# Order edges for the norms' small TensorE products, and a PSUM bank for one column half, in a two-layer decoder trunk

## The chip, the cores and the metric

The kernel runs on one core of a Trainium2 chip. The metric is the device time of one execution in microseconds. Before the change the median of three runs was 1242.19 us (1241.92 to 1243.76).

## The reference

The model has two layers on 512 tokens plus 16 learned meta tokens (528 columns in all), with a model width of 1024. Everything is float32 at the interface. Each layer does, cut to what matters here:

```
h = h + rmsnorm( mixer(rmsnorm(h, pre_mix)),  post_mix )
h = h + rmsnorm( conv_ffn(rmsnorm(h, pre_ffn)), post_ffn )

mixer(x):    proj = x @ w_in  (1024 x 3600); a retention group (4 heads) and a gated
             linear attention group (4 heads) work on its columns;
             both results, normalised and gated, side by side, then @ w_out (1024 x 1024)
conv_ffn(x): u = x @ ffn_up (1024 x 5632); a causal width-3 convolution per column;
             (gelu(first half) * second half) @ ffn_down (2816 x 1024)
rmsnorm(x, w): x * rsqrt(mean(x*x over the width) + 1e-6) * w
```

The output is h without the meta tokens. A norm is over the width, and the width lies on the partitions in this kernel, so each token's sum of squares runs across partitions.

## The kernel before, in words

**Layout.** Activations are kept transposed: 8 tiles of 128 rows (the width), with the 528 tokens along the columns. Columns are cut into two halves, 0 to 232 and 232 to 528 (`SPLIT` is 232; the second half has 296 columns). In the last layer the first half begins at column 14 for what only the tokens' own outputs need, so it has 218 columns.

**Large products.** A float32 product is made of three fp16 products: weights and activations are split into a high and a low part, and `product_step` issues high*high (L469), high*low (L470) and low*high (L471) into the same PSUM accumulator. `product` runs `product_step` over the 8 row tiles (22 in the down-projection). An accumulator is one tile of a pool of three PSUM banks (`mm`); a second pool (`mx`) has the other five. The profile names these accumulators `pj` (input projection), `po` (output projection), `pu` (up-projection), `pp` (paired up-projection) and `pd` (down-projection). The rank-16 gate projection has its own step, `rank_step` (L727). Weights come by DMA into a stage and are split by ScalarE (L120) and VectorE (L124), about ten units ahead of their use.

**Norms.** `norms` runs once for each column half behind the output projections of both layers and behind the first layer's down-projection: six times. While the product's tiles are evacuated, `sumsq` squares them on ScalarE and adds the squares (L435, GpSimd or VectorE) into `acc`, 128 partitions of partial sums. Then `token_rstd` works in two small steps on TensorE:

- `nst` (L419): two or three products of a slice of `acc` with a column of ones give each token's sum; VectorE scales it and adds epsilon (L402), GpSimd raises it to the power -0.5 (L403);
- `nbc` (L643): VectorE makes a diagonal of the result (`ndg`, L647), and a product of ones with this diagonal spreads it over all partitions.

In fp32 each such product shows as two in the profile (four or six in a group). Between the two calls of `token_rstd`, eight passes on VectorE (L448), GpSimd (L450) and ScalarE add the normalised result to the residual `h` and collect the squares of the new `h`. After the second call, `scaled` and `split` write the next stage's input `xh` (`every` in the profile): its high part by ScalarE (L407), its low part by VectorE (L408). So a norm has four small groups on TensorE, in a chain with the other engines between them.

**What sets the order.** The first part of the kernel (to the first nine tiles of the first mixer) is in a region whose order is that of the program. Behind it, a planner writes each engine's order before the run. It goes by its own model of durations, and each time an engine is free in that model it takes, among the instructions whose inputs the model calls ready, the one that stands first in the program. In the program, a half's `norms` is written out whole as soon as that half's products are: so the four small groups stand before all the products of the next half, and the planner puts each where its model has its input ready. On the chip every engine then works strictly through the written order.

**The last block.** The last down-projection (`last_down`) works on blocks of 128 tokens and 512 output columns with a Strassen-like scheme: seven products (`w11`, `t1`, `t2`, `w22`, `t3`, `w21`, `t4`) with sums of the inputs and of the weights, into PSUM accumulators `pa`, `pb` and `pd` of one bank each (L1324). The last product, `t4`, is added to `pa[0]` for token block 2, and then to `pa[1]` for token block 3, in two column halves of 256. Behind each half, ScalarE squares it (L1392) and VectorE multiplies it with the gains (L1396). The products of the second half write the same bank that these two read, so the framework makes them wait. At the end come the scaled sum (L1397), the power (L1398), four passes of VectorE that scale and add the residual (L1401; `hp` is the residual, transposed by TensorE at L1363) and four output transfers (L1402), on SyncE's and ScalarE's queues in turn. Block 2's own end is `result` (L1342 to L1345) and `final` (L1349 to L1353).

## Time and profile before

| | |
|---|---|
| median of the runs | 1242.19 us (1241.92 to 1243.76) |
| the profiled execution's own time | 1243.79 us |
| its span in the trace | 1241.7 us |
| TensorE busy (matmuls) | 1221.0 us, 98% |
| VectorE busy | 838.9 us, 68% |
| ScalarE busy | 667.5 us, 54% |
| GpSimd busy | 160.0 us, 13% |
| share of TensorE in the chain that ended last | 90% |

PE is TensorE (PEld its weight loads), DVE VectorE, ACT ScalarE, POOL GpSimd, SP SyncE; a q behind a name is the engine's sequencer. A timeline row gives the start, the duration, the engine and line, the operation, the output and input tiles, the shape and the count of instructions merged into it; a bracket at its end gives the engine's idle time before it and what ended that. A row of the waits gives the engine and line, what it waited for, the total in us, how often, and the longest. Matmuls overlap, so the duration of one (0.29 us for 296 columns) is longer than the distance to the next.

### The profile page before, as it was taken

What the parts mean: (1) busy time and instruction counts of PE and PEld (TensorE: products, weight loads), DVE (VectorE), ACT (ScalarE), POOL (GpSimd) and SP (SyncE); (2) the same over time, 40 slices, a digit from 0 to 9 for tenths busy, and PEclk for the clock granted to TensorE, in tenths of its full rate; (3) what the DMA queues carried; (4) which work ended last, traced back from release to release, by engine and by line L of the source; (5) the groups of instructions that cost most, each with busy time, mean ns of one, the idle gap of its engine ahead of it and who ended that gap; (6) DMA issues with size and microseconds to landing.
All of it is one profiled execution on the core that took longest, in us unless ns stands there. A gap on an engine that the chain in (4) does not pass through costs nothing.

```text
span 1241.7 us, 26411 instructions
## 1 busy us (share of the span) xinstructions
PE 1221.0 (98%) x11079; PEld 1013.5 (82%) x11079; DVE 838.9 (68%) x1485; ACT 667.5 (54%) x1316; POOL 160.0 (13%) x205
## 2 busy tenths in 40 slices
PE   8999999999999999999999999999999999999997
PEld 7778888988888888988887788889798888886444
DVE  5677745467998777623465777443769768887686
ACT  5674445454776666523335654453648556664442
POOL 1012311153000000000220223011520000000001
PEclk9999999999999999999999999999999999999999
DMA  7932121131423333424243232212314333304461
GB/s 202 273 102 86 60 79 52 52 97 40 136 70 110 100 97 96 119 73 108 63 114 98 69 86 70 69 52 69 104 51 136 102 103 103 119 2 170 160 239 68
DMA packets 207275, 124.18 MB, mean 100 GB/s; under 512 B 6880, under 2 KB 194836, under 8 KB 207156
## 3 DMA queue, kind: packets, MB, share of 16 engines
q1 hardware_dynamic: 206708, 121.71, 33.7%
q8 instruction: 87, 1.43, 0.5%
q0 software_dynamic: 160, 0.52, 0.1%
q14 instruction: 32, 0.26, 0.1%
q10 hardware_dynamic: 288, 0.26, 0.1%
HBM read 120.38 MB, written 2.10 MB: 99 GB/s over the span
## 4 chain that ended last, share of the span: by engine, by line
PE 90%; ACT 3%; DVE 3%; issue 1%; POOL 1%; DMA 0%; SPq 0%; POOLq 0%; DVEq 0%; ACTq 0%
PE pu L470 11%; PE pu L471 11%; PE pu L469 11%; PE pl L1324 8%; PE pj L469 7%; PE pj L471 7%; PE pj L470 7%; PE pp L1145 3%; PE pd L470 3%; PE pd L471 3%; PE pd L469 3%; PE po L469 2%; PE po L471 2%; PE po L470 2%; PE o L776 1%
## 5 line engine op out<-in xcount | busy, mean ns | idle before, releaser
L470 PE MATMUL pu<-every,unit 128*128 128x296 f16 (+2 forms) x1248 | 341.2, 274 | 2.1 <-DVE every L408 2.1
L471 PE MATMUL pu<-every,unit 128*128 128x296 f16 (+2 forms) x1248 | 341.2, 274 | 0.0
L469 PE MATMUL pu<-every,unit 128*128 128x296 f16 (+2 forms) x1248 | 339.6, 274 | 0.7 <-ACT every L407 0.7
L471 PEld LDWEIGHTS <-unit 128*128 128x128 f16 x2700 | 264.4, 98 | 44.2 <-issue 3.8
L469 PEld LDWEIGHTS <-unit 128*128 128x128 f16 x2700 | 264.6, 98 | 43.9 <-issue 3.9
L470 PEld LDWEIGHTS <-unit 128*128 128x128 f16 x2700 | 264.8, 98 | 39.0 <-issue 0.6
L124 DVE SCALAR_TENSOR_TENSOR unit<-st,unit 128x1024 f16<-128x1024 f32 (+1 forms) x173 | 212.0, 1227 | 100.7 <-ACT unit L120 100.0
L471 PE MATMUL pj<-every,unit 128*128 128x296 f16 (+2 forms) x888 | 244.8, 276 | 0.9 <-DVE unit L124 0.9
L469 PE MATMUL pj<-every,unit 128*128 128x296 f16 (+2 forms) x888 | 245.1, 276 | 0.5 <-DVE room L933 0.5
L470 PE MATMUL pj<-every,unit 128*128 128x296 f16 (+2 forms) x888 | 244.9, 276 | 0.0
L120 ACT ACTIVATE unit<-st 128x1024 f16<-128x1024 f32 (+1 forms) x171 | 177.9, 1041 | 75.1 <-PE pu L471 21.2
L1201 ACT ACTIVATE u<-pu 128x296 f32<-128x296 f32 (+2 forms) x156 | 58.5, 378 | 72.6 <-PE pu L471 72.6
L435 DVE TENSOR_TENSOR acc<-acc,sq 128x296 f32<-128x296 f32 (+2 forms) x60 | 33.4, 558 | 77.6 <-ACT sq L433 75.7
L471 PE MATMUL pd<-av,unit 128*128 128x232 f16 (+1 forms) x308 | 84.7, 276 | 0.0
L470 PE MATMUL pd<-av,unit 128*128 128x232 f16 (+1 forms) x308 | 84.7, 276 | 0.0
L469 PE MATMUL pd<-av,unit 128*128 128x296 f16 (+1 forms) x308 | 84.5, 276 | 0.0
L403 POOL TENSOR_TENSOR every<-every 128x5 f32<-128x5 f32 (+6 forms) x31 | 38.1, 1229 | 295.7 <-DVE every L402 250.4
L1324 PE MATMUL pl<-unit,fk 128*128 128x512 f16 x330 | 71.4, 379 | 0.0
L1190 DVE SCALAR_TENSOR_TENSOR cg<-u,every,cg 128x527 f32<-128x527 f32 (+1 forms) x88 | 66.4, 754 | 5.0 <-ACT cg L1185 4.3
L471 PE MATMUL po<-merged,unit 128*128 128x296 f16 (+2 forms) x256 | 69.7, 274 | 0.0
L470 PE MATMUL po<-merged,unit 128*128 128x296 f16 (+2 forms) x256 | 69.7, 274 | 0.0
L469 PE MATMUL po<-merged,unit 128*128 128x296 f16 (+2 forms) x256 | 69.4, 274 | 0.0
(260 smaller groups left out, 1745.7 us busy)
## 6 DMA issues: line engine op xcount, KB each, us to landing
st<-in_ffn_up SPq DMA_DIRECT2D x78, 512.0 KB, 3.8
st<-in_w_in SPq DMA_DIRECT2D x56, 512.0 KB, 4.6
st<-in_ffn_down SPq DMA_DIRECT2D x46, 512.0 KB, 3.9
st<-in_w_out SPq DMA_DIRECT2D x16, 512.0 KB, 3.6
st<-in_ffn_up SPq DMA_DIRECT2D x20, 256.0 KB, 4.0
st<-in_ffn_down SPq DMA_DIRECT2D x8, 384.0 KB, 3.4
xt<-in_x SPq DMA_DIRECT2D x6, 256.0 KB, 6.2
w<-in_ffn_down SPq DMA_DIRECT2D x3, 512.0 KB, 4.3
```

The source lines that it names most:

```text
L120: self.kern.nc.scalar.activation(self.u[:, 0], self.st, AF.Copy, scale=SW)
L124: self.kern.nc.vector.scalar_tensor_tensor(out=self.u[:, 1, ks], in0=self.st[:, ks], scalar=SW, in1=self.u[:, 0, ks], op0=ALU.mult, op1=AL ...
L403: nc.gpsimd.tensor_tensor(out=r[:w, :n], in0=t[:w, :n], in1=self.mhalf[:w, :n], op=ALU.pow)
L435: eng.tensor_tensor(out=acc[:, :n], in0=acc[:, :n], in1=sq[:, :n], op=ALU.add)
L469: nc.tensor.matmul(ps[:, :n], w[:, 0, kk, :], x[:, 0, n0:n1], start=first, stop=False)
L470: nc.tensor.matmul(ps[:, :n], w[:, 0, kk, :], x[:, 1, n0:n1], start=False, stop=False)
L471: nc.tensor.matmul(ps[:, :n], w[:, 1, kk, :], x[:, 0, n0:n1], start=False, stop=last)
L776: nc.tensor.matmul(o[:, i, :], intra(i), vn(i), start=i == 0, stop=i == 0, skip_group_check=i > 0)
L1145: mm = lambda p, q, **kw: nc.tensor.matmul(ps, u[:, p, k, :], x[k][:, q], skip_group_check=more, **kw)
L1190: nc.vector.scalar_tensor_tensor(out=to, in0=u[:, max(lo, d) - d : L - d], scalar=self.cvec[:, ci(i) : ci(i) + 1], in1=to, op0=ALU.mult, o ...
L1201: nc.scalar.activation(u[:, n0:n1], ps[:, : n1 - n0], AF.Copy, scale=IXW)
L1324: mm = lambda x, w, **kw: nc.tensor.matmul(ps[:, cols], x, w[:, cols], skip_group_check=more, **kw)
```

## The change

Two edits.

*Marks.* A clock counts the columns of the large products in the order of the program: `product_step` adds three times its columns, `rank_step` its columns. At the start of `norms`, four places on this clock are set: 2.2, 3.5, 2.6 + 66*n/2340 and 3.5 us apart, at 2340 columns per us, where n is the half's number of columns. When the clock has passed a place, the first matmul of that `product_step` gets an edge to the last matmul of the small group that belongs to the place: it must come behind it in TensorE's order. The edge is for the planner; it makes no semaphore.

*The last block.* The first column half of `t4` for token block 3 goes to a bank of its own, `pe`, the third of the pool `mm`. What `pa[1]` held in these columns is copied to SBUF beforehand (`done`) and added by VectorE when the half is evacuated. The square of this half is taken from SBUF, and its product with the gains is a pass of its own. The order of the last few steps is written anew: the scaled sum and the power come before the last half's product with the gains, and the last passes are one of 512 columns and two of 256, with three output transfers.

```diff
+PER_US = 2340
...
         self.gated, self.credit, self.beat = [], [0.0, 0.0], 0
+        self.clock, self.marks = 0.0, []
...
-    def token_rstd(self, acc, n0, n1, out):
+    def token_rstd(self, acc, n0, n1, out, at_sum, at_spread):
...
         for i, c0 in enumerate(at):
-            nc.tensor.matmul(st[:w, i : i + 1], acc[:, c0 : c0 + w], self.ones[:, :1], start=True, stop=True)
+            one = nc.tensor.matmul(st[:w, i : i + 1], acc[:, c0 : c0 + w], self.ones[:, :1], start=True, stop=True)
+        self.marks.append((at_sum, one))
         r = self.rstd(st[:w, :nk], nk, 1.0 / D, EPS, w)
         yield
         bc = self.mx([P, WN], "nbc")
         for i, c0 in enumerate(at):
-            self.spread(bc[:, c0 : c0 + w], r[:w, i : i + 1], w)
+            one = self.spread(bc[:, c0 : c0 + w], r[:w, i : i + 1], w)
+        self.marks.append((at_spread, one))
         out.append(bc)
...
-        yield from self.token_rstd(acc, n0, n1, out)
+
+        at, ways = [self.clock], (PER_US * 2.2, PER_US * 3.5, PER_US * 2.6 + 66 * n, PER_US * 3.5)
+        for way in ways:
+            at.append(at[-1] + way)
+        yield from self.token_rstd(acc, n0, n1, out, at[1], at[2])
...
-        yield from self.token_rstd(acc2, n0, n1, out)
+        yield from self.token_rstd(acc2, n0, n1, out, at[3], at[4])
...
+    def after_marks(self, ins, n):
+
+        while self.marks and self.marks[0][0] <= self.clock:
+            self.tc.add_manual_dep(ins.ins, self.marks.pop(0)[1].ins.name,
+                                   mybir.DependencyInfo(mybir.DependencyClass.NoSync, mybir.DependencyReason.DATA), reason="marks")
+        self.clock += n
+
     def product_step(self, ps, w, kk, x, n0, n1, first, last):
         nc = self.nc
         n = n1 - n0
-        nc.tensor.matmul(ps[:, :n], w[:, 0, kk, :], x[:, 0, n0:n1], start=first, stop=False)
+        one = nc.tensor.matmul(ps[:, :n], w[:, 0, kk, :], x[:, 0, n0:n1], start=first, stop=False)
+        self.after_marks(one, 3 * n)
...
     def rank_step(self, ps, u, k, n0, n1):
         for i in range(2):
+            self.clock += n1 - n0
...
+        done = self.g([P, 512], F32, "part")[:, :256]
+        nc.scalar.activation(done, pa[1][:, :256], AF.Copy, scale=IAW)
+        pe = self.mm([P, 512], "pl")
         pd = banks(self.mx)
         multiply(("w21", av["x12"], pd, False))
...
-        half, sums = [slice(0, 256), slice(256, 512)], self.ss
-        for i, cols in enumerate(half):
-            multiply(("t4", av["x22"], {1: pa[1]}, True), cols=cols)
-            sq = self.g([P, 512], F32, "sqo")[:, cols]
-            nc.scalar.activation(sq, pa[1][:, cols], AF.Square, scale=IAW, accum_out=sums[:, i : i + 1])
-            if i == 0:
-                nc.vector.tensor_tensor(out=sums[:, 2:3], in0=sums[:, 0:1], in1=ss[:, 7:8], op=ALU.add)
-                nc.vector.tensor_scalar(out=sums[:, 3:4], in0=sums[:, 2:3], scalar1=1.0 / D, scalar2=EPS, op0=ALU.mult, op1=ALU.add)
-            nc.vector.scalar_tensor_tensor(out=ys[3][0][:, cols], in0=pa[1][:, cols], scalar=IAW, in1=gbc[0][:, cols], op0=ALU.mult, op1=ALU.mult)
+        first, last = slice(0, 256), slice(256, 512)
+        y, sums = ys[3], self.ss
+        multiply(("t4", av["x22"], {1: pe}, False), cols=first)
+        nc.vector.scalar_tensor_tensor(out=y[0][:, first], in0=pe[:, first], scalar=IAW, in1=done, op0=ALU.mult, op1=ALU.add)
+        sq = self.g([P, 512], F32, "sqo")
+        nc.scalar.activation(sq[:, first], y[0][:, first], AF.Square, accum_out=sums[:, 0:1])
+        nc.vector.tensor_tensor(out=y[0][:, first], in0=y[0][:, first], in1=gbc[0][:, first], op=ALU.mult)
+        nc.vector.tensor_tensor(out=sums[:, 2:3], in0=sums[:, 0:1], in1=ss[:, 7:8], op=ALU.add)
+        nc.vector.tensor_scalar(out=sums[:, 3:4], in0=sums[:, 2:3], scalar1=1.0 / D, scalar2=EPS, op0=ALU.mult, op1=ALU.add)
+        multiply(("t4", av["x22"], {1: pa[1]}, True), cols=last)
+        sq = self.g([P, 512], F32, "sqo")
+        nc.scalar.activation(sq[:, last], pa[1][:, last], AF.Square, scale=IAW, accum_out=sums[:, 1:2])
         nc.vector.scalar_tensor_tensor(out=sums[:, 4:5], in0=sums[:, 1:2], scalar=1.0 / D, in1=sums[:, 3:4], op0=ALU.mult, op1=ALU.add)
         nc.gpsimd.tensor_tensor(out=sums[:, 5:6], in0=sums[:, 4:5], in1=self.mhalf[:, :1], op=ALU.pow)
-        for i in (1, 0):
-            for j, cols in enumerate(half):
-                nc.vector.scalar_tensor_tensor(out=ys[3][i][:, cols], in0=ys[3][i][:, cols], scalar=sums[:, 5:6], in1=hps[3][i][:, cols], op0=ALU.mult, op1=ALU.add)
-                (nc.scalar if j else nc.sync).dma_start(self.a["out"][0, P * 3 : P * 4, 512 * i + 256 * j : 512 * i + 256 * (j + 1)], ys[3][i][:, cols])
+        nc.vector.scalar_tensor_tensor(out=y[0][:, last], in0=pa[1][:, last], scalar=IAW, in1=gbc[0][:, last], op0=ALU.mult, op1=ALU.mult)
+        for i, c0, n in ((1, 0, 512), (0, 0, 256), (0, 256, 256)):
+            cols = slice(c0, c0 + n)
+            nc.vector.scalar_tensor_tensor(out=y[i][:, cols], in0=y[i][:, cols], scalar=sums[:, 5:6], in1=hps[3][i][:, cols], op0=ALU.mult, op1=ALU.add)
+            (nc.scalar if n < 512 and c0 == 0 else nc.sync).dma_start(self.a["out"][0, P * 3 : P * 4, 512 * i + c0 : 512 * i + c0 + n], y[i][:, cols])
```

More of the change, by code (lines that the diff above doesn't have):

```diff
@@ L642, in spread @@
         nc = self.nc
-        nc.tensor.matmul(out, self.ones[:w, :], self.diagonal(r, w), start=True, stop=True)
+        return nc.tensor.matmul(out, self.ones[:w, :], self.diagonal(r, w), start=True, stop=True)
     def diagonal(self, r, w):
```

## The prediction

> **What bounds the kernel now.** I read the page first, then TensorE's waits, then each place the change touches in order of time.
>
> ```profile
> span 1241.7 us, 26411 instructions
> PE 1221.0 (98%) x11079; PEld 1013.5 (82%) x11079; DVE 838.9 (68%) x1485; ACT 667.5 (54%) x1316; POOL 160.0 (13%) x205
> PEclk9999999999999999999999999999999999999999
> ```
> TensorE is busy 98% of the span at full granted clock. No part of the change takes a product away, so it can only win idle time of TensorE, or time after its last product. Who that idle time waits for:
>
> ```profile
> PE pu L470 <- DVE every L408: 2.1, 4, 0.6
> PE pl L1324 <- DVE every L402: 1.8, 1, 1.8
> PE pj L727 <- ACT every L407: 0.9, 1, 0.9
> PE pu L469 <- ACT every L407: 0.7, 1, 0.7
> PE pj L727 <- DVE every L408: 0.7, 1, 0.7
> ```
> Rows 1, 3, 4 and 5 are the starts of stages that need the normalised activations (split at L407 and L408): 4.4 us, which is all the marks can win. Row 2 is the last block: 1.8 us.
>
> **Part one: the marks.** They add no work. An edge makes one large product follow a small one in TensorE's order, without a semaphore. Site A, the norm behind the first out-projection's first column half (232 columns), on TensorE:
>
> ```profile
> 253.46 0.29 PE L469 MATMUL po<-merged,unit 128*128 128x296 f16 x1
> ...
> 257.24 0.47 PE L419 MATMUL nst<-every,acc 128*116 128x1 f32 x4
> ...
> 261.59 0.60 PE L643 MATMUL nbc<-ndg,every 116*128 116x116 f32 x4
> ...
> 272.98 0.47 PE L419 MATMUL nst<-every,acc 128*116 128x1 f32 x4
> ...
> 277.78 0.67 PE L643 MATMUL nbc<-ndg,every 116*128 116x116 f32 x4 [0.15 <-ACT sq L433]
> ...
> 280.43 0.46 PE L469 MATMUL pu<-every,unit 128*128 128x232 f16 x3 [0.71 <-ACT every L407]
> ```
> The second half's products start at 253.46. A group of small products lasts 0.47 us (nst) or 0.60 (nbc). Without these, the four groups stand 3.8, 7.7, 18.4 and 22.8 us of products behind 253.46 (for the third: 272.98 - 253.46 - 0.47 - 0.60). The marks stand at 2.2, 5.7, 14.84 and 18.34 us (2.2; +3.5; +2.6 + 66*232/2340; +3.5), and a step of three products is 0.38 us, so they act at 2.3, 6.1, 15.2 and 18.6. All four lie ahead of today's places, by 1.5 to 4.2 us. When the inputs are there:
>
> ```profile
> 254.56 0.40 DVE L435 TENSOR_TENSOR acc<-acc,sq 128x232 f32<-128x232 f32 x1 [17.33 <-ACT sq L433]
> 259.65 0.47 DVE L647 TENSOR_SCALAR ndg<-every 116x116 f32<-116x116 f32 x2 [0.60 <-POOL every L403]
> 271.37 1.33 DVE L435 TENSOR_TENSOR acc<-acc,sq 128x232 f32<-128x232 f32 x2
> 274.38 0.15 DVE L402 TENSOR_SCALAR every<-nst 116x2 f32<-116x2 f32 x1
> 275.08 1.68 POOL L403 TENSOR_TENSOR every<-every 116x2 f32<-116x2 f32 x1
> 276.80 1.03 DVE L647 TENSOR_SCALAR ndg<-every 116x116 f32<-116x116 f32 x2 [0.59 <-POOL every L403]
> ```
> The first two groups stand later than they must (254.96 against 257.24, 260.12 against 261.59): 2.3 and 1.5 us. The last two have no slack (272.70 against 272.98; 277.83, where TensorE waits 0.15).
>
> Does an edge on one product really pull the small group forward? The planner takes whatever it counts as ready, highest in program order first, across up to three accumulators:
>
> ```profile
> 660.99 0.29 PE L727 MATMUL pj<-every,unit 128*128 128x296 f16 x1 [0.87 <-ACT every L407]
> 661.12 0.41 PE L469 MATMUL pj<-every,unit 128*128 128x296 f16 x2
> ```
> Here, as at 280.43 (three L469 in a row, where one accumulator would run L469, L470, L471), two other accumulators take their turn when one's next step waits. So at a mark I expect the next tiles' products to run in the gap, and the small group to stay where the planner counts it ready, except where the half runs out of other tiles. By counting tiles of 24 products (0.1265 us each, 296/2340) that happens in the two out-projections, before the last group: at A tile 5 waits for the third group, tile 6's second step for the fourth; 171 products stand ahead of it instead of 182 (counted in the trace), 11 * 0.1265 = 1.4 us earlier. Site E, the second layer's out-projection (218 columns), by the same count: 14 products, 1.8 us. Its waits from 890 to 900 us, and GpSimd there:
>
> ```profile
> PE pu L470 <- DVE every L408: 1.0, 2, 0.6
> ```
> ```profile
> 887.95 3.43 POOL L435 TENSOR_TENSOR acc<-acc,sq 128x296 f32<-128x296 f32 x2
> 891.34 0.70 POOL L403 TENSOR_TENSOR every<-every 109x2 f32<-109x2 f32 x1
> ```
> If VectorE, ScalarE and GpSimd keep their times, these become waits, but the products held back then cover the later waits: A +1.4 - 1.6 = -0.2 (its waits are 0.15 at nbc, 0.71 at 280.43, and 2.1 - 1.0 = 1.1 at L470, 1.9 together, of which I leave 0.3); E +1.8 - 1.0 = +0.8. Against that, GpSimd's power (L403) now stands behind sums of the other half (L435). At E it starts when two sums of 3.43 us together are done; the tiles held back deliver their sums later, so the power can go first: up to 1.7 us at E (half of the 3.43), at A 0.55 (275.08 against 274.53) and, if VectorE's weight work steps back too, 0.9 (L402 at 274.38 against nst's end at 273.45). That makes A as good as -0.2 - 1.2 = -1.4 (the late steps I left keep 0.25) and E 0.8 - 1.3 = -0.5 (likewise 0.4). I take the middle of each: A -0.8, E +0.15. The norms behind second halves (marks 1.5 us or less ahead of today's places, tiles to spare) I take at +0.15, for sums that close a little later on GpSimd. The down-projection's tiles are 66 products long, so others always stand ready: nothing. Marks in all: **-0.5 us**. The cover named here is the free choice of tiles; if it is gone, rivals one and two hold.
>
> **Part two: the last block.** Times around its last column half, by engine:
>
> ```profile
> 1231.65 3.76 PE L1324 MATMUL pl<-unit,m 128*128 128x256 f16 x33 [1.75 <-DVE every L402]
> ```
> ```profile
> 1232.38 1.41 DVE L1352 SCALAR_TENSOR_TENSOR yo<-yo,every,hp 128x512 f32<-128x512 f32 x2 [0.66 <-POOL every L403]
> 1235.50 0.38 ACT L1392 ACTIVATE sqo<-pl 128x256 f32<-128x256 f32 x1 [4.73 <-PE pl L1324]
> 1236.01 0.42 DVE L1396 SCALAR_TENSOR_TENSOR yo<-pl,every 128x256 f32<-128x256 f32 x1 [2.22 <-ACT sqo L1392]
> 1236.35 0.15 DVE L1397 SCALAR_TENSOR_TENSOR every<-every 128x1 f32<-128x1 f32 x1
> 1236.58 0.54 POOL L1398 TENSOR_TENSOR every<-every 128x1 f32<-128x1 f32 x1 [4.23 <-DVE every L1397]
> 1237.15 1.66 DVE L1401 SCALAR_TENSOR_TENSOR yo<-yo,every,hp 128x256 f32<-128x256 f32 x4 [0.65 <-POOL every L1398]
> ```
> The 33 products wait 1.75 us for readers of their own bank. With the first half in another bank nothing holds them: **-1.75**, and TensorE ends near 1233.7. The sum for the power (L1397) moves ahead of the 0.42 us product with the gains (L1396), which then runs under GpSimd's 0.54 us: 1236.35 - 1236.01 = **-0.34**. Four last passes (1.66) become one of 512 and two of 256: 1.41 / 2 + 2 * 1.66 / 4 = 1.54, **-0.1**; four output transfers become three, the last alone on SyncE's queue, whose earlier one is issued some 0.8 us (two of these passes) before. What is added: a 0.38 us copy on ScalarE (`done`), early, beside products; one VectorE pass more in the first half (at most 0.42), beside the 33 products. VectorE is free at 1232.38 + 1.41 = 1233.79, and ScalarE's square with its sum, done 0.60 us behind the last product today (1235.41 to 1236.01), comes at about 1234.2, so it just fits; without that cover 0.4 is lost. Sum: **-2.2**, between -1.8 and -2.3.
>
> **Sum.** The profiled execution lasted 1243.79 us, 2.1 more than its span, and 1.6 above the median of 1242.19; I carry the difference over: -2.2 - 0.5 = -2.7, so 1242.19 - 2.7 = **1239.5**.
>
> **Rivals.** *One: the order is strict and the chains keep up.* If no other tile steps in, every small group moves to its mark; where its input is early (A's first two), results come 1.5 us earlier and more at each link, and the 4.4 us at the stage starts go. I leave 0.8 for links that are tight: -2.2 - 3.6, **1236.4**. For it: the slack of 2.3 and 1.5. Against: the three accumulators above.
>
> *Two, slower: the order is strict and the chains do not keep up.* At A, the second nst's input comes 272.70 - 261.59 = 11.1 us behind the first nbc, the mark only 0.6 + 9.1 behind it: 1.4 of wait; then 277.83 - 272.98 = 4.85 against 0.47 + 3.4: 1.0 more. At its end 1.9 is won back: +0.5. The down-projection has no wait to win back:
>
> ```profile
> 610.15 0.60 PE L643 MATMUL nbc<-ndg,every 116*128 116x116 f32 x4
> 621.56 0.77 DVE L435 TENSOR_TENSOR acc<-acc,sq 128x232 f32<-128x232 f32 x2
> ```
> 12.2 us (622.33 - 610.15) against 9.7: +2.5. E by A's sum: +0.5. Behind the second halves the square sum closes late,
>
> ```profile
> 284.08 0.45 DVE L435 TENSOR_TENSOR acc<-acc,sq 128x296 f32<-128x296 f32 x1
> ```
> 284.53, against a mark 2.4 us behind the first product of the next stage at 280.43: up to 1.7; with the same at E's second half 3.4, of which I take 2.4, since xh comes sooner there too. Together 5.9 - 2.2 = +3.7, **1245.9**. It decides from 4.7 us of waits on (2.2 + 2.5). The Trainium skill ("TensorE: Matmul & The Clock Gate", Part 2: What happens when you issue a matmul) says that matmuls stay in program order and only weight loads are pulled ahead; the trace agrees at 277.78, and by that rule each mark that is early costs its whole wait.
>
> *Three: the tail gives little back.* Freed of the bank, the last half's products may be planned ahead of the last ones of block 2 (L1344 and L1345, a power, 1.41 of L1352; today its last pass ends at 1233.79, 2.1 us behind the 33 products' start), and VectorE is then late for the end: up to 1.9 of the 2.2 lost. With the marks -0.5: **1241.4**.
>
> **Chances.** Forecast 0.46 (own range 1238.3 to 1241.0), one 0.20, two 0.13, three 0.21. A measurement of this kernel can tell about 0.2%, 2.5 us: faster is under 1239.7, slower over 1244.7. Faster: 0.28 of the forecast's and all of one, 0.48. Slower: 0.10 of two. Same: 0.42. The range reaches to rival one and most of the way to two: 1236.0 to 1243.8.
>
> **What would show it.** The wait of 1.75 us at L1324 gone, and from the last product to the first last pass about 1.4 us instead of 1.74 (1235.41 to 1237.15). At A, nst still 3.8 us and nbc still 7.7 us of products behind the half's start (forecast) or 2.3 and 6.1 (one and two). Waits in front of L419 and L643 beyond 0.3 us each point to two; pu and pj waits gone without these, to one. I am wrong if the small groups moved and the time did not, or if the new order opens waits elsewhere, in the mixer for instance, that no row here names.

## The result, and the profile after

The changed kernel took 1253.57 us (median of four runs, 1252.41 to 1254.99) beside 1242.97 us for the kernel before: a ratio of 1.0086, with a 95% interval of 1.0068 to 1.0103. It is slower by some 10.6 us. The forecast was 1239.5 us, and the time lies outside the predicted range, beyond even the slower rival.

The page of the changed kernel (its profiled execution: 1252.41 us):

```profile
span 1250.4 us, 26405 instructions
PE 1224.6 (98%) x11079; PEld 1015.7 (81%) x11079; DVE 839.3 (67%) x1485; ACT 669.3 (54%) x1317; POOL 160.8 (13%) x205
PEclk9999999989999999999999999999999999999999
```
The number of matmuls is the same, and TensorE is still busy 98% of the span: a page with shares alone would not show where the time went. One digit differs from before, the 8 in the ninth slice of the granted clock. TensorE's waits of the changed kernel, by what they waited for:

```profile
PE nst L421 <- DVE acc L439: 6.0, 4, 3.7
PE nbc L659 <- DVE ndg L663: 2.2, 2, 2.0
PE pu L486 <- DVE every L410: 1.2, 2, 1.0
```
Before, no row named the small products with more than 0.3 us. Now they wait 8.2 us, 3.7 of it in one piece. (Lines have moved: `nst` L419 is L421, `nbc` L643 is L659, the products L469 to L471 are L484, L486 and L487, the sums L435 are L439, the weights' split on VectorE L124 is L125, `rank_step` L727 is L744, and the last block's products L1324 are L1341.) The wait of 1.75 us in the last block has gone from the list. Sites A and E are the prediction's; B is the norm behind the second column half of A's out-projection. The small groups at site A, in time order on TensorE:

```profile
257.42 0.47 PE L421 MATMUL nst<-every,acc 128*116 128x1 f32 x4
...
260.02 0.60 PE L659 MATMUL nbc<-ndg,every 116*128 116x116 f32 x4
...
273.40 0.93 PE L421 MATMUL nst<-every,acc 128*116 128x1 f32 x4 [3.72 <-DVE acc L439]
...
280.81 0.60 PE L659 MATMUL nbc<-ndg,every 116*128 116x116 f32 x4
```
The third group ran at 273.40, where it had run at 272.98 before. But now only 90 products of the second half stood between the first group and it, where there had been 119 (18 and 72 against 32 and 87, counted in the trace), and 29 * 0.1255 us = 3.64 us of products were missing. That is the wait. The second and third group now stand behind whole tiles of 24 products: 30 + 18 make two tiles, and 72 more make five.

The wait is not the whole loss. The granted clock in steps of 3.41 us around it (columns: window, its length, then TensorE's busy time with its count of matmuls, weight loads, VectorE, ScalarE, GpSimd, granted clock, DMA share, GB/s):

```profile
268.50:271.91 3.41, 1.18 (x10) 0.69 (x7) 3.20 (x4) 3.00 (x7) 2.03 (x3) 1.00 0.53 154
271.91:275.32 3.41, 1.92 (x9) 1.51 (x10) 2.28 (x5) 0.00 (x0) 0.71 (x1) 0.50 0.46 139
275.32:278.74 3.42, 3.42 (x16) 2.11 (x14) 1.37 (x3) 0.00 (x0) 2.56 (x3) 0.50 0.58 167
...
288.98:292.39 3.41, 1.91 (x19) 1.63 (x19) 1.27 (x4) 0.36 (x1) 1.89 (x2) 1.00 0.88 253
292.39:295.80 3.41, 3.41 (x20) 2.61 (x18) 0.63 (x3) 0.36 (x1) 0.27 (x1) 0.50 0.10 29
...
667.86:671.27 3.41, 1.99 (x15) 1.29 (x15) 3.41 (x9) 2.51 (x7) 0.00 (x0) 1.00 0.00 0
```
Behind the wait the clock was at half for 6.8 us, and again for 3.4 us behind two shorter waits at B (0.99 and 0.81 us). TensorE is then "busy" with half as many products (16 in 3.42 us, where a full-clock window holds some 29). The stretches show as busy time, so no list of waits has them.

The end, on ScalarE, VectorE and GpSimd:

```profile
1243.06 0.19 ACT L1419 ACTIVATION_READ_ACCUMULATOR sqo<-pl 128x1 f32 x1
1243.12 1.40 DVE L1369 SCALAR_TENSOR_TENSOR yo<-yo,every,hp 128x512 f32<-128x512 f32 x2
...
1244.50 0.41 DVE L1422 SCALAR_TENSOR_TENSOR yo<-pl,every 128x256 f32<-128x256 f32 x1
1244.83 0.15 DVE L1420 SCALAR_TENSOR_TENSOR every<-every 128x1 f32<-128x1 f32 x1
...
1245.63 1.53 DVE L1425 SCALAR_TENSOR_TENSOR yo<-yo,every,hp 128x512 f32<-128x512 f32 x3 [0.65 <-POOL every L1421]
```
The last square is summed at 1243.25, but VectorE has block 2's final passes (L1369) in front of it, and takes the product with the gains (L1422) ahead of the sum for the power (L1420). From TensorE's last product (1242.74) to the first last pass it is 2.89 us, against 1.74 before.

**The ledger.** The same sum can be made for every profiled execution: TensorE's idle time from its first to its last instruction; half of the busy time that fell into half-clock stretches, which is what these cost; the time from its last product to the end; and the rest, which is the products themselves (and 1.0 us ahead of the first).

| profiled execution | span | idle | half clock | behind the last product | rest |
|---|---|---|---|---|---|
| before | 1241.7 | 13.5 | 1.7 | 6.3 | 1220.3 |
| changed kernel | 1250.4 | 17.2 | 4.4 | 7.6 | 1221.2 |
| tail_only | 1239.5 | 11.0 | 0 | 7.6 | 1220.9 |
| marks_only | 1251.4 | 18.4 | 4.6 | 6.3 | 1222.0 |
| late_third | 1250.0 | 14.6 | 6.8 | 7.6 | 1221.0 |
| fill_the_wait | 1252.9 | 15.0 | 6.3 | 7.6 | 1223.9 |
| last_pair_only | 1252.7 | 15.4 | 8.2 | 7.6 | 1221.4 |
| four_banks_mid_tile | 1246.9 | 14.5 | 0 | 8.2 | 1224.2 |
| four_banks_first_step | 1257.9 | 20.4 | 4.9 | 8.2 | 1224.3 |
| tail_ordered | 1238.0 | 10.8 | 0 | 6.2 | 1221.0 |
| places_by_trace | 1236.2 | 9.0 | 0 | 6.2 | 1221.0 |
| places_by_trace_2 | 1233.7 | 7.6 | 0 | 6.2 | 1219.9 |

The rest lies between 1219.9 and 1222.0 us in all kernels with three banks but fill_the_wait, which has 2.8 us of products more. Between before and the changed kernel, 3.7 + 2.7 + 1.3 + 0.9 = 8.6 us. In idle, the last block gave 1.75 us back, so the marks cost 5.5 us of idle time, and 2.7 us of half clock stand beside it: 4.4 at A and B, less 1.7 that the kernel before had elsewhere. The medians are 10.6 us apart and not 8.6 because the profiled execution of the changed kernel is its fastest, and that of the kernel before one of its slowest.

### The profile page after: what moved, and what is told of

Its sections match the earlier page's. It is cut to its first block, busy times and chain, and to the rows that moved or that the text cites. A ratio compares the mean times of both kernels' runs of the same rounds, so it can differ in the third digit from the quotient of the medians.

```text
span 1250.4 us, 26405 instructions
## 1 busy us (share of the span) xinstructions
PE 1224.6 (98%) x11079; PEld 1015.7 (81%) x11079; DVE 839.3 (67%) x1485; ACT 669.3 (54%) x1317; POOL 160.8 (13%) x205
## 5 line engine op out<-in xcount | busy, mean ns | idle before, releaser
L486 PE MATMUL pu<-every,unit 128*128 128x296 f16 (+2 forms) x1248 | 342.6, 275 | 1.2 <-DVE every L410 1.2
L487 PE MATMUL pu<-every,unit 128*128 128x296 f16 (+2 forms) x1248 | 342.7, 275 | 0.0
L484 PE MATMUL pu<-every,unit 128*128 128x296 f16 (+2 forms) x1248 | 342.1, 275 | 0.0
L484 PEld LDWEIGHTS <-unit 128*128 128x128 f16 x2700 | 265.7, 98 | 43.2 <-issue 2.8
L487 PEld LDWEIGHTS <-unit 128*128 128x128 f16 x2700 | 264.8, 98 | 44.1 <-issue 2.6
L486 PEld LDWEIGHTS <-unit 128*128 128x128 f16 x2700 | 264.8, 98 | 39.1 <-issue 0.6
L125 DVE SCALAR_TENSOR_TENSOR unit<-st,unit 128x1024 f16<-128x1024 f32 (+1 forms) x173 | 211.2, 1223 | 103.4 <-ACT unit L121 103.1
L487 PE MATMUL pj<-every,unit 128*128 128x296 f16 (+2 forms) x888 | 244.2, 275 | 0.9 <-DVE unit L125 0.9
L484 PE MATMUL pj<-every,unit 128*128 128x296 f16 (+2 forms) x888 | 244.5, 276 | 0.5 <-DVE room L950 0.5
L486 PE MATMUL pj<-every,unit 128*128 128x296 f16 (+2 forms) x888 | 244.3, 275 | 0.0
L439 DVE TENSOR_TENSOR acc<-acc,sq 128x296 f32<-128x296 f32 (+2 forms) x60 | 34.6, 578 | 75.8 <-ACT sq L437 74.1
L487 PE MATMUL pd<-av,unit 128*128 128x232 f16 (+1 forms) x308 | 84.7, 276 | 0.0
L486 PE MATMUL pd<-av,unit 128*128 128x232 f16 (+1 forms) x308 | 84.7, 276 | 0.0
L484 PE MATMUL pd<-av,unit 128*128 128x296 f16 (+1 forms) x308 | 84.5, 276 | 0.0
L405 POOL TENSOR_TENSOR every<-every 128x5 f32<-128x5 f32 (+6 forms) x31 | 35.2, 1137 | 293.9 <-DVE every L404 254.7
L1341 PE MATMUL pl<-unit,fk 128*128 128x512 f16 x330 | 71.4, 379 | 0.0
L486 PE MATMUL po<-merged,unit 128*128 128x296 f16 (+2 forms) x256 | 70.7, 278 | 0.0
L487 PE MATMUL po<-merged,unit 128*128 128x296 f16 (+2 forms) x256 | 70.5, 278 | 0.0
L484 PE MATMUL po<-merged,unit 128*128 128x296 f16 (+2 forms) x256 | 70.5, 278 | 0.0
```

Source lines behind the costliest of these rows:

```text
L125: self.kern.nc.vector.scalar_tensor_tensor(out=self.u[:, 1, ks], in0=self.st[:, ks], scalar=SW, in1=self.u[:, 0, ks], op0=ALU.mult, op1=AL ...
L405: nc.gpsimd.tensor_tensor(out=r[:w, :n], in0=t[:w, :n], in1=self.mhalf[:w, :n], op=ALU.pow)
L439: eng.tensor_tensor(out=acc[:, :n], in0=acc[:, :n], in1=sq[:, :n], op=ALU.add)
L484: one = nc.tensor.matmul(ps[:, :n], w[:, 0, kk, :], x[:, 0, n0:n1], start=first, stop=False)
L486: nc.tensor.matmul(ps[:, :n], w[:, 0, kk, :], x[:, 1, n0:n1], start=False, stop=False)
L487: nc.tensor.matmul(ps[:, :n], w[:, 1, kk, :], x[:, 0, n0:n1], start=False, stop=last)
```

## The experiments

Two questions: what each part does alone, and why the marks cost what they cost. Theory W in the first four expectations is that the changed kernel's third group was put too early, so that TensorE stands still until VectorE delivers.

**tail_only and marks_only: each part alone.** The first leaves the edges out:

```diff
         while self.marks and self.marks[0][0] <= self.clock:
-            self.tc.add_manual_dep(ins.ins, self.marks.pop(0)[1].ins.name,
-                                   mybir.DependencyInfo(mybir.DependencyClass.NoSync, mybir.DependencyReason.DATA), reason="marks")
+            self.marks.pop(0)
```
The second is the changed kernel with the last block of before.

> The change's last block alone: the clock runs on, but no edge is written. Theory W (the loss comes from waits of TensorE ahead of the small groups, and from the half clock that follows them): nothing of the 9 us is left, and the last block gives back little, because VectorE does block 2's last passes between the last product and the power: about -0.6 us against the kernel before. My prediction's sum for this part was -2.2. Rival O (any new order of this kernel costs several us, wherever it comes from): +3 or more.

> The change's marks alone, with the last block of before. Theory W: all of the loss and a little more, +9.2 us against before (the offset between the two traces just ahead of the last block). Rival O would also give a loss, but no fixed one.

Measured beside 1242.63 us: tail_only 1241.39 us, ratio 0.9991 (0.9982 to 1.0000); marks_only 1254.13 us, ratio 1.0094 (1.0080 to 1.0108). So the loss is the marks' (11.5 us by the medians and 9.7 by the profiled executions, where 9.2 were expected), and the last block gains about 1 us (0 to 2.2 by the interval) instead of 2.2. In the ledger the last block alone has 2.5 us less idle time, with the 1.75 us in it, and 1.3 us more behind the last product. The waits of marks_only:

```profile
PE nst L421 <- DVE acc L439: 6.0, 4, 3.7
PE nbc L659 <- DVE ndg L663: 2.3, 2, 2.0
PE pl L1341 <- DVE every L404: 1.8, 1, 1.8
```
They are those of the changed kernel, with the last block's 1.75 us as before.

**late_third: the third place later.** It is 4.3 us later on the clock behind first halves, and the fourth moves with it:

```diff
-        at, ways = [self.clock], (PER_US * 2.2, PER_US * 3.5, PER_US * 2.6 + 66 * n, PER_US * 3.5)
+        at, ways = [self.clock], (PER_US * 2.2, PER_US * 3.5, PER_US * 2.6 + 66 * n + self.later_by(n), PER_US * 3.5)
...
+    def later_by(self, n):
+        return PER_US * 4.3 if n < 296 else 0
```

> The whole change, with the third place of the clock 4.3 us later behind first halves; the other places keep their distances, so the fourth is later too. Theory W: the wait of 3.7 us ahead of the third small group behind the first out-projection and the half clock after it go; what is left is under 2 us of shorter waits; -6 to -9 us against the changed kernel. Rival O: within 2 us of the changed kernel, since as many instructions are reordered.

Measured: 1252.18 us, ratio 1.0074 (1.0061 to 1.0088), 1.4 us under the changed kernel's median, not 6 to 9, and the two intervals overlap. The expectation failed. The third group on TensorE, and below it the windows:

```profile
273.67 0.69 PE L421 MATMUL nst<-every,acc 128*116 128x1 f32 x4 [1.87 <-DVE acc L439]
```
```profile
270.56:273.97 3.41, 1.54 (x13) 1.03 (x12) 3.31 (x4) 0.58 (x2) 2.47 (x3) 1.00 0.28 80
273.97:277.38 3.41, 3.41 (x16) 2.17 (x16) 2.59 (x5) 1.81 (x3) 1.43 (x2) 0.50 0.65 187
284.21:287.62 3.41, 2.15 (x20) 1.77 (x20) 3.41 (x9) 1.41 (x5) 0.00 (x0) 1.00 0.34 98
287.62:291.04 3.42, 3.42 (x21) 2.68 (x19) 1.57 (x7) 0.53 (x2) 1.06 (x1) 0.50 0.27 81
...
690.40:693.81 3.41, 1.94 (x25) 1.41 (x24) 1.77 (x2) 3.41 (x7) 0.00 (x0) 1.00 0.04 12
693.81:697.22 3.41, 3.41 (x15) 2.10 (x16) 3.38 (x7) 0.98 (x2) 0.00 (x0) 0.50 0.08 15
```
The wait fell to 1.87 us, since 95 products now stood between the second group and the third. But the sums came at 273.61 instead of 273.35, and 1.87 us was still enough to be followed by half clock. The next 32 products then took 6.1 us to the fourth group (273.67 to 279.78), so the second half's operands were late, TensorE waited for them (0.63, 0.33 and 1.23 us), and a second stretch at half clock came behind that. In the ledger 2.6 us less idle time stand against 2.5 us more half clock. But one of the four windows at half clock, the one from 693.81, can't be put down to the marks: it follows a wait of 1.47 us in the second layer's mixer (`ptl` waits for ScalarE's `gv`), which the changed kernel has too, with full clock behind it.

What one site costs can be read by the alignment of two traces: the start of the same large product is compared in both, against a kernel without marks (tail_ordered). A and B together cost 8.2 us in the changed kernel and 5.6 here, so the later place did win 2.6 us there. Against that, 1.7 us were lost at 693.81, and E cost 3.9 us instead of 2.6. Theory W was too simple in two ways: it took the sums' time as fixed, and it had no price for the clock beyond A.

**fill_the_wait: products in place of the wait.** 22 extra products into a scratch bank that nobody reads, between the second and third group of A:

```diff
+        if len(self.fill) < 22 and self.filled:
+            self.filled = False
+            ps2 = self.scratch
+            for _ in range(22):
+                f = nc.tensor.matmul(ps2[:, :n], w[:, 0, kk, :], x[:, 0, n0:n1], start=True, stop=True)
...
```

> The whole change, plus 22 products (2.8 us, a repeat of one that is there, into a bank that nobody reads) placed in TensorE's order just ahead of the third small group behind the first out-projection, where it waits 3.72 us. They are work that the kernel before does not do. Theory W with the half clock: the group still waits for its sum until the same time, but TensorE stays busy, the clock is not halved from 272 to 279 us, and the time falls by 3.4 us, or 5.1 if the second stretch at half clock (292 to 296) goes as well. Rival (only the wait costs, the half clock in the records is an effect without a price): no change against the changed kernel.

Measured: 1252.57 us, ratio 1.0074 (1.0059 to 1.0090), 1.0 us under the changed kernel's median, with overlapping intervals: the time decides for neither theory. On TensorE, then VectorE and GpSimd:

```profile
269.75 2.93 PE L496 MATMUL fill<-merged,unit 128*128 128x296 f16 x22
...
274.56 0.57 PE L422 MATMUL nst<-every,acc 128*116 128x1 f32 x4 [1.88 <-DVE acc L440]
```
```profile
272.59 1.92 DVE L440 TENSOR_TENSOR acc<-acc,sq 128x232 f32<-128x232 f32 x2
```
```profile
271.83 2.42 POOL L440 TENSOR_TENSOR acc<-acc,sq 128x296 f32<-128x296 f32 x2 [0.25 <-ACT sq L438]
```
The wait should have fallen by 2.8 us to 0.9; it fell to 1.88, because the last sums ended 1.2 us later than in the changed kernel (274.51 against 273.35). The last two sums took 1.92 us, where they take 0.89 in the changed kernel, and GpSimd was adding squares of the second half at the same time, where it is idle in the changed kernel (late_third has the same 1.92 us). In all twelve traces VectorE's sums of this shape take 0.39 to 0.40 us while GpSimd is idle, and mostly 0.69 to 1.05 beside its work. No run changes that alone.

A half-clock window still followed (275.34 to 278.75), one instead of two. By the alignment, A and B cost 6.1 us with the added 2.8 us of products in them, against 8.2. The waits there are only 2.3 us shorter, less than the added products, so the 2.7 us of half clock that are gone must have had a price: the rival does not fit. The whole time hides this, because windows at half clock came elsewhere: 1.7 us at 695.18 behind the same wait in the mixer, and 2.9 us at E, where the waits are those of the changed kernel.

**last_pair_only: which pair of marks costs.** The first two marks of every norm make no edge:

```diff
-        yield from self.token_rstd(acc, n0, n1, out, at[1], at[2])
+        yield from self.token_rstd(acc, n0, n1, out, None, None)
```
(with `if at_sum is not None` and `if at_spread is not None` ahead of the two appends).

> Kernel: the changed kernel without the edges of each norm's first two marks; the third and fourth keep theirs. Planned order at the first out-projection 30, 32, 58 and 35 products (before 30, 32, 87 and 33; changed 30, 18, 72 and 35), and 72 instead of 100 ahead of the third group of the norm after it. Question: which pair costs. Theory (the third edge takes products from ahead of a group whose sums VectorE delivers at 272.7 us anyway): 29 products less of 0.1255 us each, so a wait of 3.4 us at the third group of the first out-projection, some 2 us at the norm after it, 2 to 4 us at the fourth group of the second out-projection, and two to four stretches of half clock of 1.7 us each: 1249 to 1255. Rival (the early first pair costs, since it moves the weights' splits on VectorE into the sums' way; the third only seems to): as the run of the last block alone, 1241 to 1244.

Measured beside 1243.57 us: 1252.84 us, ratio 1.0074 (1.0058 to 1.0090), as the theory said. Its waits:

```profile
PE nst L421 <- DVE acc L441: 6.0, 3, 3.3
PE nbc L661 <- ACT sq L439: 2.0, 1, 2.0
```
3.26 us at A's third group (expected 3.4), 1.87 behind it at B (expected some 2), 1.97 at E's fourth (expected 2 to 4), and three stretches of half clock, five windows long in sum. The second pair alone makes nearly the whole loss; the first is not needed for it. No run has the first pair alone.

**four_banks_mid_tile and four_banks_first_step: when is an edge passed?** Both have four banks for the products' accumulators instead of three. They differ only in where an edge goes that would fall on a tile's first step:

```diff
-        while self.marks and self.marks[0][0] <= self.clock:
+        while not first and self.marks and self.marks[0][0] <= self.clock:
```

> Kernel: the changed kernel with a fourth bank for the products' accumulators (one less for the small tiles), and an edge that would fall on a tile's first step is put on its second. Step under test: the prediction's 'the next tiles' products run in the gap'. Planned order at the first out-projection: groups at 30, 30, 90 and 21 products, against 30, 18, 72 and 35 of the changed kernel. Theory (an edge on a tile's first step holds every later tile too, since accumulators are handed out in program order; one inside a tile is passed as long as an accumulator is free): the 3.72 us wait for the sums is gone, because 120 products stand ahead of them as in before; 1.5 to 2 us may come back at the fourth group, which stands at 21. Time 1242 to 1247. Rival (edges cost by their number or by the wait on semaphores, wherever they are): 1252 to 1255 as the changed kernel.

> Kernel: the changed kernel with the same fourth bank, its edges where the diff has them (the second and third on first steps). Planned order 30, 18, 72 and 35 as in the changed kernel. Theory: 1252 to 1255, the 3.7 us wait stays and with it the half clock. Rival (it was the lack of a bank, not the first step): as four_banks_mid_tile.

Measured: 1248.63 us (ratio 1.0052, 1.0037 to 1.0067) and 1259.62 us (1.0141, 1.0127 to 1.0155). Both are slower than expected, by something they share: their rest in the ledger is 3 us above the others', and the regrouped banks bring waits elsewhere, 2.8 us of them in front of the out-projections (row `po L484 <- ACT gr L1024`). What was to be told apart is the difference, 11.0 us. First the kernel with edges on first steps, then the one with edges inside the tile:

```profile
PE nst L421 <- DVE acc L439: 6.0, 4, 3.7
```
```profile
PE nbc L659 <- DVE ndg L663: 2.3, 2, 1.6
```
With the edges inside the tiles no row of the waits names the sums, and the trace has no half clock before the end; what came back is 1.55 us at A's fourth group and 0.72 at E's, as expected. In the ledger the pair differs by 5.9 us of idle time and 4.9 of half clock, 10.8 of the 11.0. The written order shows how: an edge inside a tile is passed by the tiles that have a bank, and the small group stays late; an edge on a tile's first step is not passed. The products ahead of the groups one to four at A:

| kernel | one | two | three | four |
|---|---|---|---|---|
| before | 30 | 32 | 87 | 33 |
| changed kernel, four_banks_first_step | 30 | 18 | 72 | 35 |
| late_third | 30 | 18 | 95 | 32 |
| last_pair_only | 30 | 32 | 58 | 35 |
| four_banks_mid_tile | 30 | 30 | 90 | 21 |
| places_by_trace | 15 | 24 | 87 | 32 |

That it is the handing out of banks in program order which makes a first step strict is an argument from the code, not shown by a run of its own.

**tail_ordered: the last block with its products in order.** The last block alone, and one edge more: the last half's first product follows the last ones of block 2's column and of the first half.

```diff
-        multiply(("t4", av["x22"], {0: pa[0]}, True))
+        ends = multiply(("t4", av["x22"], {0: pa[0]}, True))
...
-        multiply(("t4", av["x22"], {1: pe}, False), cols=first)
+        ends += multiply(("t4", av["x22"], {1: pe}, False), cols=first)
...
-        multiply(("t4", av["x22"], {1: pa[1]}, True), cols=last)
+        multiply(("t4", av["x22"], {1: pa[1]}, True), cols=last, after=ends)
```

> Kernel: no marks; the new last block, with one more edge: the first product of the last half comes after the last products of block 2's column and of the first half. Step under test: that VectorE is done with block 2's final passes when ScalarE's last square ends. In the changed kernel and in the run of the last block alone, some products of the last half stand ahead of block 2's last ones, and the stretch from the last product to the first of the last passes took 2.89 us instead of 1.74. Theory (the planned order of the last products makes VectorE late, nothing else): with the edge the stretch is 1.3 to 1.8 us again, the wait of 1.75 us stays gone, so about 2 us below the kernel before and 1 to 1.5 us below the last block alone (ratio 0.998 to 0.9988). Rival (block 2's passes are late by their own length, whatever the order of the products): the stretch stays at 2.6 to 3 us and the time at that of the last block alone.

Measured beside 1242.46 us: 1240.55 us, ratio 0.9989 (0.9981 to 0.9998).

```profile
1230.85 1.40 DVE L1374 SCALAR_TENSOR_TENSOR yo<-yo,every,hp 128x512 f32<-128x512 f32 x2
...
1232.10 0.20 ACT L1424 ACTIVATION_READ_ACCUMULATOR sqo<-pl 128x1 f32 x1
...
1232.42 0.16 DVE L1425 SCALAR_TENSOR_TENSOR every<-every 128x1 f32<-128x1 f32 x1
1232.50 0.42 DVE L1427 SCALAR_TENSOR_TENSOR yo<-pl,every 128x256 f32<-128x256 f32 x1
...
1233.23 1.53 DVE L1430 SCALAR_TENSOR_TENSOR yo<-yo,every,hp 128x512 f32<-128x512 f32 x3 [0.32 <-POOL every L1426]
```
VectorE is done with block 2 (L1374) at 1232.25, and the last square at 1232.30: it just fits, the sum (L1425) goes ahead of the product with the gains (L1427), and from the last product (1231.78) to the first last pass it is 1.45 us. By the ratios tail_ordered and tail_only (0.9991) can't be told apart; in the profiled executions, both without half clock, the span falls by 1.5 us (1239.5 to 1238.0).

**places_by_trace and places_by_trace_2: the same tool, with places from the trace.** If a mark costs nothing by itself, marks whose places follow the readiness of the operands should win. Places are in products; each edge is put on the next 40 steps, so that it is strict wherever it falls, and `rank_step` takes edges too.

```diff
-PER_US = 2340
+PLACES = {(1, 1): 17, (1, 2): 46, (5, 1): 17, (5, 2): 50, (4, 3): 126, (4, 4): 148}
...
-        at, ways = [self.clock], (PER_US * 2.2, PER_US * 3.5, PER_US * 2.6 + 66 * n, PER_US * 3.5)
-        for way in ways:
-            at.append(at[-1] + way)
+        self.calls += 1
+        at = [PLACES.get((self.calls, i), 0) for i in range(5)]
+        at = [place and self.clock + place * n for place in at]
```
(The key is the norm's number and the group's.) The second kernel adds `(2, 3): 142, (2, 4): 164, (6, 3): 138, (6, 4): 160`.

> Kernel: tail_ordered, and marks at three places only, counted in products from the trace of before and held by an edge on each of the next 40 product steps: at the norm behind each out-projection's first half the first sum goes from 30 products behind the half's start to 15 and the spread from 62 to 39 (second layer the same), and at the norm behind the down-projection's second half the second sum goes from 103 to 96 and its spread from 35 to 27 products. Theory (a mark costs nothing by itself; a group may stand as early as its operand is ready, and TensorE then has that much more left to do when the chain comes back): A's waits of 1.93 us, the 1.53 us ahead of the second layer's second half and the 0.99 us of the second out-projection go down by 3 us or more in sum, and with them the half-clock stretch behind them: 3 to 6 us below before, ratio 0.995 to 0.9975. Rival (VectorE's backlog sets when the sums of the second norm are ready, 272.7 us before, 273.4 us and 273.6 us with earlier spreads): the waits only move, and the time is that of tail_ordered within 1 us.

> Kernel: places_by_trace, and the second pair of marks at two more places, where its trace shows VectorE idle for 1.43 and 2.39 us ahead of the small products and TensorE waiting 0.43 and 0.89 us (first layer) and 0.35 and 0.66 us (second) for the operands that follow: third group at 93 instead of 100 products and fourth at 27 instead of 35 in the first layer's up-projection, 98 instead of 105 and 30 instead of 36 in the second's. Theory (place by the trace's readiness): 1.8 us and 1.5 us earlier, so most of the 2.3 us of waits goes: 1 to 2.3 us below places_by_trace, ratio to the kernel before 0.9948 to 0.996. Rival (VectorE's passes behind the fourth group, not its place, set the operands): no change, 0.9967.

Measured: 1238.51 us, ratio 0.9967 (0.9957 to 0.9978), and 1236.52 us beside 1243.57, ratio 0.9948 (0.9934 to 0.9961). Both came out as the theory said: the second is 6.5 us faster than the kernel before by the ratio (4.9 to 8.2 by the interval). In places_by_trace A's waits went from 1.93 to 0.27 us, the 1.53 us ahead of the second layer's second half to 0.42, and the second out-projection's 0.99 to nothing; 2.3 us came back in the two up-projections (0.43 and 0.89, 0.35 and 0.66), and of these the second kernel's four places left 0.07. A in places_by_trace:

```profile
255.23 0.47 PE L421 MATMUL nst<-every,acc 128*116 128x1 f32 x4
...
258.58 0.60 PE L664 MATMUL nbc<-ndg,every 116*128 116x116 f32 x4
...
269.96 0.47 PE L421 MATMUL nst<-every,acc 128*116 128x1 f32 x4
...
274.76 0.67 PE L664 MATMUL nbc<-ndg,every 116*128 116x116 f32 x4 [0.27 <-DVE ndg L668]
```
The third group runs 3.0 us earlier than before and waits for nothing. VectorE's rows show how the sums could come earlier here and not in the changed kernel. The changed kernel, between its second and third group:

```profile
262.41 1.46 DVE L125 SCALAR_TENSOR_TENSOR unit<-st,unit 128x1024 f16<-128x1024 f32 x1
...
266.65 1.70 DVE L125 SCALAR_TENSOR_TENSOR unit<-st,unit 128x1024 f16<-128x1024 f32 x1
...
270.71 1.83 DVE L125 SCALAR_TENSOR_TENSOR unit<-st,unit 128x1024 f16<-128x1024 f32 x1
272.46 0.89 DVE L439 TENSOR_TENSOR acc<-acc,sq 128x232 f32<-128x232 f32 x2
```
and places_by_trace:

```profile
261.44 1.35 DVE L125 SCALAR_TENSOR_TENSOR unit<-st,unit 128x1024 f16<-128x1024 f32 x1
...
265.73 1.70 DVE L125 SCALAR_TENSOR_TENSOR unit<-st,unit 128x1024 f16<-128x1024 f32 x1
...
267.35 2.33 DVE L441 TENSOR_TENSOR acc<-acc,sq 128x232 f32<-128x232 f32 x4
```
VectorE works almost without a pause in this stretch, so the sums come when its queue has been worked off. In the changed kernel three splits of weights (5.0 us) stand between the second group's passes and the last sums, here two (3.05 us): the second group comes 1.4 us earlier still, and its passes stand ahead of a split. The kernel before and last_pair_only have two splits there as well. In these three the sums end 11.1 us behind the start of the second group, in the changed kernel 13.3. That the splits are the cause is read from these rows; no run moves a split alone.

## Why the prediction was wrong, and where it was right

**"At a mark I expect the next tiles' products to run in the gap."** This step failed, and with it the sum. It held where an edge fell inside a tile: A's first group stayed at 30 products, 3.8 us as predicted, and the down-projection's groups stayed near their places without a wait, as "nothing" said. It failed where an edge fell on a tile's first step: A's second (18 instead of 32) and third group (72 instead of 87), E's second (18 instead of 32) and fourth (3 instead of 34), and the first group of both norms behind the second halves (24 products of the next stage ahead of it at B, instead of 39). The evidence I read, other accumulators taking turns at 280.43 and 660.99, shows them passing a product that waits inside a tile already begun, not one that waits at a tile's first step. I did not ask where in its tile each mark falls, though the clock's step counts were all there.

**A -0.8.** Measured at A and B together: +3.85 us of waits (3.72, 0.26, 0.99 and 0.81 against 1.93) and about 4.4 us of half clock; 8.2 us by the alignment of the two traces between 250 and 320 us. The part on GpSimd did come: the power (L405) started 0.1 us behind VectorE's scaling. It did not help, since the sums were what was late.

**E +0.15.** By the same alignment +2.6 us: waits of 0.51, 1.96 and 0.94 against 0.59 and 0.40. **Second halves +0.15:** their first groups wait 0.81 and 0.94 us, which are in these sums.

**Rival two** had the mechanism (the order is strict and the chains do not keep up) but not its size, and I gave it 0.13. Its wait of 1.4 us at A took the 11.1 us from the second group to the sums as fixed and the third place as 9.7 behind it. The place was right (9.7 us: 72 products, 9.0, and the group's own 0.6), but the chain became 13.3 us (260.02 to 273.35), with a split more on VectorE in it. Its 2.5 us in the down-projection didn't come, since there the marks fell inside tiles and were passed. The Trainium skill ("TensorE: Matmul & The Clock Gate", Part 2: What happens when you issue a matmul) says that matmuls stay in program order; by that rule an early mark costs its whole wait, and the trace agrees at 273.40.

**"TensorE is busy 98% of the span at full granted clock."** This was wrong in a way that the row of 9s hides: a slice of the page is 31 us, and 3.4 us at half leave it at 0.94, a 9. Before:

```profile
659.23:662.64 3.41, 1.88 (x14) 1.18 (x14) 3.07 (x8) 2.19 (x7) 0.00 (x0) 1.00 0.00 0
662.64:666.06 3.42, 3.42 (x16) 2.13 (x15) 3.42 (x10) 1.96 (x5) 0.00 (x0) 0.50 0.02 5
```
So 1.7 us of the profiled execution were half clock, behind waits of 0.87 and 0.66 us, and no term of my sum, nor of rival two, had a price for what follows a wait.

**Last block -2.2.** The -1.75 came (the row is gone), the last passes went from 1.66 to 1.53 us as said. "It just fits" failed in the changed kernel and held in tail_ordered: with the products in order, the stretch is 1.45 us, and the gain 1.9 us by the medians (0.2 to 2.4 by the interval). **Rival three** named the mechanism, the last half's products ahead of block 2's last ones: behind the last two of block 2 run only 23 products of 256 columns, where the last half has 33. Its price was 1.9 us; it was 1.4 (2.89 - 1.45), of which 0.33 is L1422 ahead of L1420, the reverse of the order in the diff.

## What to carry to other kernels

An edge that pulls small work forward is free only if the work left ahead of it lasts until its input is there: take the place from the input's readiness in the trace, see what the engine that makes the input has in its queue, and check in the written order whether the edge is strict, since it can be passed inside a tile and be absolute at its start. In this kernel, price 1.8 us or more of waiting in one window of 3.41 us at its length plus 1.7 us for each half-clock window behind it. The same kind of edge lost 10 us and more at places from a formula, and at places from the trace won 2.7 to 5.1 us beyond the last block's gain (0.9967 and 0.9948 against 0.9989).

## What the runs showed of the hardware

**Short waits are followed by half clock, one window of 3.41 us at a time.** The stretches of one run lie on a grid: 271.91 and 292.39 in the changed kernel are 20.48 us apart, six times 3.413. All windows in which TensorE stood 1.8 us or more were followed by one, those with 2.2 or more by two, windows with 1.3 to 1.8 us some times (one of them, 893.15 in fill_the_wait with 1.52, by two). The limit is not settled: 1.91 us busy at 288.98 was followed by half clock and 1.99 at 667.86 was not, but late_third has it behind 2.15 and before has full clock behind 1.66 (1229.26 to 1232.67).

**The same waits cost 1.7 us or nothing, by where they fall on the grid.** The row of before above has 0.87 and 0.66 us in one window. tail_only has 0.87 and 0.65 us at the same place:

```profile
657.76:661.17 3.41, 2.54 (x23) 2.13 (x22) 1.55 (x4) 1.33 (x4) 0.00 (x0) 1.00 0.00 0
661.17:664.59 3.42, 2.77 (x22) 2.03 (x21) 3.42 (x10) 1.63 (x6) 0.00 (x0) 1.00 0.02 5
```
Here they lie on both sides of a boundary, and the clock stays full. So a single profile can differ by 1.7 us from another of the same kernel: of tail_only's 2.2 us against before in the span, 1.7 are this. It fits that the runs of the kernel before beside these experiments lie at 1241.4 to 1242.6 us with a granted clock of 0.999, or at 1243.4 to 1245.5 us with 0.996 to 0.998. The Trainium skill ("TensorE: Matmul & The Clock Gate", Part 1) describes a free-running window of 3413 ns, and the trace agrees. In its section "HAM oscillation — how this bites in real kernels" it gives as the rule that idle gaps over about 3.4 us are what to avoid; here 1.53 us in a window was enough in the kernel before, and 1.26 in late_third (284.21).

**Equal waits were followed by unequal half clock at other places too.** E has the same three waits in the changed kernel, marks_only and fill_the_wait (0.51 to 0.53, 1.96 and 0.94 us), and the half clock behind them cost nothing, 1.7 and 2.9 us. The mixer's 1.47 us lie in one window each time. They were followed by half clock in late_third and fill_the_wait and by full clock in the changed kernel and marks_only; why is not known. So the 2.5 and 2.0 us more of half clock that late_third and fill_the_wait have in the ledger can't be put down to their edits: 1.7 us in each stand behind the mixer's wait.
